# Two-layer hybrid backbone step: layer 1's gates as columns, activation quarters from the halves, four feed-forward chunks

## The chip, the cores and the metric

The kernel runs on 1 core of one Trainium2 chip. The metric is the device time of one execution in microseconds (us). Before the change the median of 3 runs is 1839.01 us (1838.3 to 1839.42).

## The reference, cut to what matters

Two layers work on 640 tokens (128 context tokens and 512 latent tokens, five tiles of 128) of width 1024. Each group has its own conditioning vector (c_ctx and c), so each modulation exists twice.

```
mod = silu(cond) @ ada_w + ada_b            # 6 x 1024: sh_m, sc_m, g_m, sh_f, sc_f, g_f
h = rmsnorm(x, norm_mix) * (1 + sc_m) + sh_m
x = x + g_m * token_mixers(h)               # projections, two kinds of scans, w_out
h = rmsnorm(x, norm_ffn) * (1 + sc_f) + sh_f
gate, up = split(h @ w_up)                  # 2816 hidden features = 22 of 128
x = x + g_f * ((silu(gate) * up) @ w_down)
```

The two gates `g_m` and `g_f` of layer 1 are what the change makes in another place. They do not depend on the tokens.

## The kernel before, in words

**Stages.** `build` runs for each layer the mixer, `w_out` and `ffn`. The large products keep float32 accuracy: each operand is split into a high and a low part (fp32r), and three matmuls (high x high, high x low, low x high) make one. Weights come through `Stream`: SP loads 512 KB into a `raw` buffer, ACT copies the high part `wh` (L103), DVE subtracts to get the low part `wl` (L104). Four slots are cut ahead.

**Order of the work.** The Python program is the order; a scheduler then puts each engine's instructions in a fixed order. Main work yields its cost in model microseconds, and `run` (L184) steps side "lanes" by it: the lane `ada` takes one step for each `Q_ADA` of cost (3.0 in the mixer, 2.0 in `w_out`, 4.0 in `ffn`). `finish` and `drain` run a lane to its end at once. Engines run in order, so an instruction that waits holds all behind it on its engine.

**Modulation.** `ada_cols` (L524) makes shift and scale as columns (one value per partition): for each of 16 tiles it loads 128 rows of the transposed ada_w (512 KB) and runs two DVE multiply-reduces against the broadcast silu rows (L546), 33 lane steps. The gates are needed as rows spread over all partitions, and `ada_gate` (L554) makes them: for each half of 512 columns it accumulates 8 tiles of ada_w on DVE for both conditionings (16 operations, L510 and L512), splits each result (L567 on ACT, L568 on DVE), sums over partitions with two matmuls against ones (L571, L572) and adds the bias (L574 on DVE); 25 lane steps. The mixer starts it for `g_m` after operation r2 (L1062), `ffn` at its start for `g_f` (L1202), and `ffn` needs it before the first chunk's down-projection (L1246).

**Feed-forward.** `ffn` cuts the 22 features into chunks, `CH`: (11, 11) in layer 0, (5, 5, 4, 4, 4) in layer 1. In a chunk the features' activations are made one after the other, and then the chunk's down-projection runs: columns 0 to 511 and 512 to 1023 with `cols_512` (512 wide, L1170 to L1172), and in the last chunk the second half as two `as_` passes of 256 columns (L795 to L797). After each, `x_add` multiplies by the gate row and adds to x (L1113, L1115, DVE). In layer 1 only the first two features are plain (`PLAIN`, L741 and L751); the other 20 use `seven` (L672), a Strassen-Winograd scheme with 7 products in place of 8, 84 matmuls of 320 columns, on combinations of the activation's four quarters (two token halves by two halves of the model width). `combos` (L652) makes these with four full-size additions or subtractions on DVE and splits three of them (E2, E1, E4); `combo_last` (L668) writes the fourth (E3) over a quarter of hT once the plain features have read it.

**Norm.** `norm_b` transposes a normalised tile on TensorE; `norm_c` (L601) scales, shifts and splits it into hT. For layer 1's feed-forward `norm_f` (L621) does that instead, cut at the token half (so tile 2 goes in two pieces), and keeps the unsplit quarters F that `combos` starts from.

**Buffers.** Pool B has 13 buffers, ON 4, PSUM 4 of two banks, the adaLN tiles 2.

Of the kernel before, what the change touches and what calls it, by code (L numbers as in the profile page):

```python
# [10 lines left out]
F32 = mybir.dt.float32  # L11
F32R = mybir.dt.float32r
I32 = mybir.dt.int32
AF = mybir.ActivationFunctionType
ALU = mybir.AluOpType
AX = mybir.AxisListType

P = 128
DM = 1024
KT = DM // P  # L20
NT = 5
TOK = NT * P
HALF = TOK // 2
# [4 lines left out]
NF = DFF // P  # L28
# [3 lines left out]
RAW_BUFS = 3  # L32
W_BUFS = 4
B_BUFS = 13
CH = ((11, 11), (5, 5, 4, 4, 4))
PLAIN = (NF, 2)
HK = KT // 2
LATE = "r2"
# [8 lines left out]
FAST = (0, 1, 3)  # L47
CUT = 256
Q_SCAN = 2.65
Q_ADA = (3.0, 2.0, 4.0)  # L50
ADP_BUFS = 2
BOOT_LOADS = (
    "L00 x4 L01 L10 L02 L11 L12 L13 L03 L20 x2 x3 x0 x1 L21 L30 L22 L31 L32 L33 L23 W W W "
# [94 lines left out]
class Net:  # L148
# [64 lines left out]
    def setup(self):  # L213
        nc, a = self.nc, self.a
        C = self.const
        self.x = C.tile([P, NT, DM], F32, name="x")
        self.ident = C.tile([P, P], F32, name="ident")
        self.onesr = C.tile([P, P], F32R, name="onesr")
        self.mask = C.tile([P, 5, P], I32, name="mask")
        self.rope = C.tile([P, 2, 512], F32, name="rope")  # L220
        self.ncol = C.tile([P, 8], F32, name="ncol")
        self.Dm = C.tile([P, DEPTH, NH, P], F32, name="Dm")
        self.cols = C.tile([P, 64], F32, name="cols")
        self.adab = C.tile([P, 96], F32, name="adab")
        self.lbc = C.tile([P, 2, 8], F32, name="lbc")
        self.oml = C.tile([P, 2, 8], F32, name="oml")
        self.gt = C.tile([P, 5, 16], F32, name="gt")
        self.hp = C.tile([P, 16], F32, name="hp")
        self.ep = C.tile([P, 16], F32, name="ep")
        self.ssq = C.tile([P, NT, 4], F32, name="ssq")  # L230
        self.modc = C.tile([P, DEPTH, 2, 2, 2, 8], F32, name="modc")

        R0 = self.ON("R0")
        nc.sync.dma_start(out=R0[0:8, :P], in_=a["c_ctx"].rearrange("(k p) -> k p", p=P))
        nc.sync.dma_start(out=R0[8:16, :P], in_=a["c"].rearrange("b (k p) -> (b k) p", p=P))
        nc.scalar.dma_start(out=self.ident, in_=a["ident"])
        sr = self.B("sr", F32R)
        self.srv = sr[:, :1024].rearrange("p (k n) -> p k n", k=KT)
        nc.gpsimd.memset(self.hp, -0.5)
        nc.gpsimd.memset(sr[:, :1024].bitcast(F32), 0.0)  # L240
        nc.gpsimd.memset(self.ep, float(np.float32(math.e)))
        warm = self.sm("warm", 1)
        nc.scalar.activation(warm, self.hp[:, :1], AF.Silu)
        nc.scalar.activation(R0[0:16, :P], R0[0:16, :P], AF.Silu)
        R1 = self.R1 = self.ON("R1")
        for r, nm, n, e in ((0, "norm_mix", 16, "l (k p) -> (l k) p"), (16, "norm_ffn", 16, "l (k p) -> (l k) p"),
                            (32, "hgrn_norm", 8, "l (k p) -> (l k) p"), (40, "ret_norm", 8, "l (k p) -> (l k) p"),
                            (48, "hgrn_lb_logits", 16, "l d (k p) -> (l d k) p")):
            nc.gpsimd.dma_start(out=R1[r:r + n, :P], in_=a[nm].rearrange(e, p=P))
        nc.gpsimd.dma_start(out=R1[:96, P:2 * P], in_=a["ada_b"].rearrange("l (k p) -> (l k) p", p=P))  # L250
        self.lgx = C.tile([P, 16], F32, name="lgx")
        nc.gpsimd.dma_start(out=self.lgx, in_=bass.AP(a["ret_decay_logit"].tensor, 0, [[0, P], [1, 16]]))
        nc.gpsimd.dma_start(out=self.ncol, in_=a["ncol"])
        pt = self.ps("pt")
        nc.tensor.transpose(pt[:, :16], R0[:16, :P], self.ident[:16, :16])
        self.sTt = C.tile([P, 16], F32, name="sTt")
        nc.vector.tensor_copy(self.sTt, pt[:, :16])
        self.sT = self.sTt.rearrange("p (c k) -> p c k", c=2)
        skc = self.sTt.rearrange("p (c k) -> p k c", c=2)
        nc.vector.tensor_copy(self.srv[:, :, 0:2], skc)  # L260
        nc.vector.tensor_tensor(self.srv[:, :, 2:4], skc, self.srv[:, :, 0:2].bitcast(F32), op=ALU.subtract)
        self.sel = C.tile([P, 2], F32, name="sel")
        nc.vector.tensor_tensor(self.sel, self.ident[:, 0:2], self.ident[:, 2:4], op=ALU.add)
# [260 lines left out]
    def ada_cols(self, l, m, alloc):  # L524
        V = self.nc.vector
        if self.srow is None:
            self.ada_rows()
            for _ in range(4):
                yield
            for c in range(2):  # L530
                self.pin(self.nc.scalar.activation(self.srow[c], self.srow[c], AF.Silu))  # L531
        tiles = [(which, j) for which in (1, 0) for j in range(KT)]

        def load(which, j):
            w = alloc("adt")
            row = 3072 * m + which * 1024 + j * P
            self.nc.sync.dma_start(out=w[:, :DM], in_=self.a["ada_t"][l, row:row + P])
            return w
        nxt = load(*tiles[0])
        for i, (which, j) in enumerate(tiles):  # L540
            w = nxt
            if i + 1 < len(tiles):
                nxt = load(*tiles[i + 1])
            yield
            for c in range(2):
                r = V.tensor_tensor_reduce(out=self.junk, in0=w[:, :DM], in1=self.srow[c], scale=1.0, scalar=0.0,  # L546
                                           op0=ALU.mult, op1=ALU.add,
                                           accum_out=self.modc[:, l, m, 1 - which, c, j:j + 1])
                if c == 0:
                    self.pin(r)  # L550
            yield
        self.mod_fin(l, m)

    def ada_gate(self, l, m, alloc, out):  # L554
        nc, a = self.nc, self.a
# [44 lines left out]

    def norm_c(self, t, src, l, m):  # L601
        nc = self.nc
        if m == 1 and PLAIN[l] < NF:
            return self.norm_f(t, src, l, m)
        km = KT // 2
        c = 0 if t == 0 else 1
        full = self.ON("full")
# [10 lines left out]
            nc.scalar.copy(hi[:, a:b], fv[:, a:b])  # L618
            nc.vector.tensor_tensor(lo[:, a:b], fv[:, a:b], hi[:, a:b].bitcast(F32), op=ALU.subtract)

    def norm_f(self, t, src, l, m):  # L621
        nc = self.nc
        c = 0 if t == 0 else 1
        sv = src[:, :DM].rearrange("p (k n) -> p k n", k=KT)
        G, S = self.modc[:, l, m, 0, c], self.modc[:, l, m, 1, c]
        a = 0
        while a < P:
            h = (t * P + a) // HALF
            b = min(P, (h + 1) * HALF - t * P)
            n, o = b - a, t * P + a - h * HALF  # L630
            for kh in range(2):
                if (h, kh) not in self.F:
                    self.F[h, kh] = self.B("hf")
                fv = self.F[h, kh].rearrange("p (k n) -> p k n", k=HK)[:, :, o:o + n]
                ks = slice(HK * kh, HK * kh + HK)
                if kh == 0:
                    for k in range(HK):
                        nc.scalar.activation(fv[:, k], sv[:, k, a:b], AF.Identity, bias=S[:, k:k + 1],
                                             scale=G[:, k:k + 1])
                else:  # L640
                    bc = lambda v: v[:, ks].unsqueeze(2).to_broadcast([P, HK, n])
                    nc.vector.tensor_tensor(fv, sv[:, ks, a:b], bc(G), op=ALU.mult)
                    nc.vector.tensor_tensor(fv, fv, bc(S), op=ALU.add)
                hi, lo = (self.hT[:, d, ks, t * P + a:t * P + b] for d in range(2))
                nc.scalar.copy(hi, fv)
                nc.vector.tensor_tensor(lo, fv, hi.bitcast(F32), op=ALU.subtract)
            a = b

    def quarter(self, h, kh):
        return [self.hT[:, d, HK * kh:HK * kh + HK, h * HALF:(h + 1) * HALF] for d in range(2)]  # L650

    def combos(self):  # L652
        V, F = self.nc.vector, self.F
        V.tensor_tensor(F[1, 0], F[1, 1], F[1, 0], op=ALU.subtract)
        V.tensor_tensor(F[0, 0], F[0, 0], F[1, 0], op=ALU.add)
        V.tensor_tensor(F[1, 1], F[0, 0], F[1, 1], op=ALU.subtract)
        V.tensor_tensor(F[0, 1], F[0, 0], F[0, 1], op=ALU.subtract)
        self.E = {}
        for n, q in ((2, (0, 0)), (1, (1, 0)), (4, (0, 1))):
            self.E[n] = [self.B("eh", F32R).rearrange("p (k t) -> p k t", k=HK) for _ in range(2)]  # L660
            self.combo(q, *self.E[n])
# [374 lines left out]
    def mixer(self, l, mid):  # L1036
# [3 lines left out]
        for i, op in enumerate(ORDER):  # L1040
# [18 lines left out]
                ch = self.ret_chain(l, j, QR, vr[nm], on[nm])  # L1059
            self.chains.append(((l, k, j), ch))  # L1060
            if op == LATE:
                self.lanes.append(((l, "gm"), self.ada_gate(l, 0, self.B, self.g_m)))  # L1062
        self.on = [on[n] for n in ("a0", "a1", "b0", "b1")]
        self.oT = [None] * KT
        for u in range(4):
# [133 lines left out]
    def ffn(self, l, mid):  # L1199
        nc = self.nc  # L1200
        self.g_f = []
        self.lanes.append(((l, "gf"), self.ada_gate(l, 1, self.ON, self.g_f)))  # L1202
        if l + 1 < DEPTH:
            for m in range(2):
                self.lanes.append(((l + 1, "c", m), self.ada_cols(l + 1, m, self.ON)))
        f0 = 0
        for ci, nch in enumerate(CH[l]):
# [209 lines left out]
```

## Time and profile before

| | us |
|---|---|
| median of 3 runs | 1839.01 |
| the profiled execution, its own time | 1836.8 |
| its span (first to last instruction) | 1835.0 |
| PE busy | 1767.5 (96%) |
| PE weight load busy | 1676.0 (91%) |
| DVE busy | 1215.7 (66%) |
| ACT busy | 764.0 (42%) |
| mean granted TensorE clock | 0.992 |

PE is TensorE's matmuls, PEld its weight loads, DVE VectorE, ACT ScalarE, SP the engine that issues most DMAs. A row of a group gives count, busy time and the mean of one, and behind the bar the idle time of its engine just before it. A timeline row gives start, duration, engine, line and operation; in brackets stands the idle time before it and who ended it. Matmuls overlap, so the distance of two starts is what one costs, and the duration is longer.

### The profile page before, as it was taken

How to read it: one execution, taken by the hardware profiler on the slowest of the kernel's cores; microseconds unless marked ns; L12 is line 12 of the kernel's file. 1: busy time of each engine (PE TensorE's matmuls, PEld its weight loads, DVE VectorE, ACT ScalarE, POOL GpSimd, SP SyncE). 2: the span in 40 equal slices, each digit the busy share in tenths (PEclk: the TensorE clock that was granted, in tenths of full speed). 3: DMA queues.
4: the chain of work that ended last, by engine and by line, in shares of the span. 5: the costliest groups of instructions: out<-in, count | busy, mean ns of one | idle time of the engine just before them, and what ended most of it. 6: DMA issues, size and time to landing. Idle time of an engine off the chain costs nothing.

```text
span 1835.0 us, 29181 instructions
## 1 busy us (share of the span) xinstructions
PE 1767.5 (96%) x11956; PEld 1676.0 (91%) x11956; DVE 1215.7 (66%) x1905; ACT 764.0 (42%) x1302; POOL 50.6 (3%) x59
## 2 busy tenths in 40 slices
PE   7999999999999999999999999999997799999997
PEld 5999999999999989999999999999896699889896
DVE  6787959755754555554466574776487676777776
ACT  7685545533422112222265464564353133233242
POOL 1100000000000000000000000000000000000000
PEclk9999999999999999999999999999999899999999
DMA  9424232222533444444222112322232223132231
GB/s 341 149 64 132 89 105 94 85 86 59 157 109 110 137 142 129 138 132 132 81 81 64 50 55 69 122 76 76 58 104 92 69 66 101 52 104 69 75 98 58
DMA packets 204358, 184.06 MB, mean 100 GB/s; under 512 B 7376, under 2 KB 171184, under 8 KB 204224
## 3 DMA queue, kind: packets, MB, share of 16 engines
q1 hardware_dynamic: 199328, 179.67, 31.1%
q10 hardware_dynamic: 4640, 2.43, 0.4%
q8 instruction: 94, 1.54, 0.3%
q14 instruction: 40, 0.33, 0.1%
q0 software_dynamic: 256, 0.09, 0.0%
HBM read 177.44 MB, written 4.72 MB: 99 GB/s over the span
## 4 chain that ended last, share of the span: by engine, by line
PE 78%; DVE 12%; ACT 5%; issue 3%; DMA 1%; POOL 1%; SPq 0%; DVEq 0%; POOLq 0%; ACTq 0%
PE gw L751 24%; PE ga L1170 6%; PE ga L1172 6%; PE ga L1171 6%; PE ga L797 4%; PE ga L796 4%; PE ga L795 4%; PE pl L888 3%; PE sx L684 2%; PE sx L685 2%; PE sx L686 2%; DVE wl L104 2%; PE sy L684 2%; PE sy L685 2%; PE sy L686 1%
## 5 line engine op out<-in xcount | busy, mean ns | idle before, releaser
L103 ACT CAST wh<-raw 128x1024 fp32r<-128x1024 f32 (+1 forms) x264 | 264.9, 1004 | 630.6 <-PE ga L1172 212.1
L104 DVE TENSOR_TENSOR wl<-raw,wh 128x1024 fp32r<-128x1024 f32 (+1 forms) x264 | 306.4, 1166 | 258.0 <-ACT wh L103 256.2
L751 PE MATMUL gw<-hT,wh 128*128 128x320 f32 x2432 | 461.9, 311 | 0.0
L751 PEld LDWEIGHTS gw<-hT,wh 128*128 128x128 f32 x2432 | 380.5, 188 | 0.6
L751 PE MATMUL gw<-hT,wl 128*128 128x320 f32 x1216 | 277.2, 309 | 0.0
L751 PEld LDWEIGHTS gw<-hT,wl 128*128 128x128 f32 x1216 | 203.1, 188 | 0.0
L795 PE MATMUL ga<-wh,hT 128*128 128x256 f32 x640 | 185.2, 289 | 0.0
L797 PE MATMUL ga<-wh,hT 128*128 128x256 f32 x640 | 181.3, 283 | 0.0
L796 PE MATMUL ga<-wl,hT 128*128 128x256 f32 x640 | 181.3, 283 | 0.0
L1170 PE MATMUL ga<-wh,act 128*128 128x512 f32 x365 | 145.2, 398 | 0.1
L1171 PE MATMUL ga<-wl,act 128*128 128x512 f32 x365 | 143.1, 392 | 0.0
L1172 PE MATMUL ga<-wh,act 128*128 128x512 f32 x365 | 141.3, 392 | 0.0
L795 PEld LDWEIGHTS ga<-wh,hT 128*128 128x128 f32 x640 | 122.5, 191 | 0.3
L796 PEld LDWEIGHTS ga<-wl,hT 128*128 128x128 f32 x640 | 122.5, 191 | 0.3
L797 PEld LDWEIGHTS ga<-wh,hT 128*128 128x128 f32 x640 | 122.3, 191 | 0.0
L546 DVE CUSTOM_DVE_ANT_0 junk<-adt,srow 128x1024 f32<-128x1024 f32 x96 | 117.1, 1220 | 1.5 <-ACT srow L531 0.2
L1113 DVE TENSOR_TENSOR xa<-ga,gate 128x512 f32<-128x512 f32 (+1 forms) x110 | 62.8, 589 | 41.6 <-PE ga L1172 17.8
L512 DVE SCALAR_TENSOR_TENSOR acc<-adw,sTt,acc 128x512 f32<-128x512 f32 x112 | 79.6, 746 | 15.2 <-DMA adw<-in_ada_w 15.2
L1170 PEld LDWEIGHTS ga<-wh,act 128*128 128x128 f32 x365 | 69.1, 189 | 18.7 <-DVE xa L1113 4.9
L1172 PEld LDWEIGHTS ga<-wh,act 128*128 128x128 f32 x365 | 69.1, 189 | 14.8
L1171 PEld LDWEIGHTS ga<-wl,act 128*128 128x128 f32 x365 | 69.1, 189 | 13.2
L684 PE MATMUL sx<-hT,wh 128*128 128x320 f32 x240 | 76.5, 322 | 3.3 <-DVE sv L694 3.0
(276 smaller groups left out, 3517.8 us busy)
## 6 DMA issues: line engine op xcount, KB each, us to landing
raw<-in_w_in SPq DMA_DIRECT2D x72, 512.0 KB, 3.8
adt<-in_ada_t SPq DMA_DIRECT2D x48, 512.0 KB, 3.8
raw<-in_w_up SPq DMA_DIRECT2D x48, 512.0 KB, 3.7
raw<-in_w_up SPq DMA_DIRECT2D x80, 256.0 KB, 3.0
raw<-in_w_down SPq DMA_DIRECT2D x39, 512.0 KB, 3.6
adw<-in_ada_w SPq DMA_DIRECT2D x64, 256.0 KB, 2.7
adw<-in_ada_w SPq DMA_DIRECT2D x16, 512.0 KB, 10.5
raw<-in_w_out SPq DMA_DIRECT2D x16, 512.0 KB, 3.7
```

Of the source, the lines that this page charges most:

```text
L103: nc.scalar.copy(hi[:, :n], raw[:, :n])
L104: nc.vector.tensor_tensor(lo[:, :n], raw[:, :n], hi[:, :n].bitcast(F32), op=ALU.subtract)
L512: nc.vector.scalar_tensor_tensor(d, w, s, d, op0=ALU.mult, op1=ALU.add)
L546: r = V.tensor_tensor_reduce(out=self.junk, in0=w[:, :DM], in1=self.srow[c], scale=1.0, scalar=0.0, op0=ALU.mult, op1=ALU.add, accum_out=s ...
L684: mm(o, hi[:, k], h[0][:, k], start=first and k == 0, stop=False, skip_group_check=True)
L751: mm(o, w[:, k], self.hT[:, d, k, sl], start=k == 0 and i == 0, stop=k == KT - 1 and i == 2)
L795: mm(o, a_hi, hi[:, j], start=i == 0, stop=False)
L796: mm(o, a_hi, lo[:, j], start=False, stop=False)
L797: mm(o, a_lo, hi[:, j], start=False, stop=i == nk - 1)
L1170: mm(o, a_hi, hi[:, j], start=i == 0, stop=False)
L1171: mm(o, a_hi, lo[:, j], start=False, stop=False)
L1172: mm(o, a_lo, hi[:, j], start=False, stop=i == nk - 1)
```

## The change

Layer 1's two gates are made in layer 0's feed-forward as columns: `ada_cols` gets two further passes (m = 2 and 3, 8 tiles each) into a new tile `gcol`. In layer 1 `gate_rows` spreads them: per conditioning 8 float32 matmuls of 128 columns, whose stationary operand is a column repeated 128 times and whose moving operand is the identity, and one ACT copy from PSUM. `ada_gate` remains for layer 0. `norm_f` is gone; `combos` makes the four quarters by adding high and low part of hT. Layer 1 has four chunks, and the `ada` lane in `ffn` steps at 3.4.

```
-CH = ((11, 11), (5, 5, 4, 4, 4))
+CH = ((11, 11), (6, 6, 5, 5))
-Q_ADA = (3.0, 2.0, 4.0)
+Q_ADA = (3.0, 2.0, 3.4)
+        self.gcol = C.tile([P, 2, 2, 8], F32, name="gcol")
@@ ada_cols
-        tiles = [(which, j) for which in (1, 0) for j in range(KT)]
+        if m >= 2:
+            m -= 2
+            tiles = [(2, j) for j in range(KT)]
+        else:
+            tiles = [(which, j) for which in (1, 0) for j in range(KT)]
...
-                                           accum_out=self.modc[:, l, m, 1 - which, c, j:j + 1])
+                                           accum_out=(self.gcol[:, m, c, j:j + 1] if which == 2 else
+                                                      self.modc[:, l, m, 1 - which, c, j:j + 1]))
...
-        self.mod_fin(l, m)
+        if which == 2:
+            b = 48 * l + 24 * m + 16
+            for c in range(2):
+                V.tensor_tensor(self.gcol[:, m, c], self.gcol[:, m, c], self.adab[:, b:b + 8], op=ALU.add)
+        else:
+            self.mod_fin(l, m)
+
+    def gate_rows(self, m, alloc, out):
+        nc = self.nc
+        for c in range(2):
+            pg = self.ps("pg")
+            for j in range(KT):
+                nc.tensor.matmul(pg[:, j * P:(j + 1) * P], self.gcol[:, m, c, j:j + 1].to_broadcast([P, P]),
+                                 self.ident, start=True, stop=True)
+            yield
+            g = alloc("gate")
+            out.append(g)
+            nc.scalar.copy(g[:, :DM], pg)
+            yield
@@ norm_c
-        if m == 1 and PLAIN[l] < NF:
-            return self.norm_f(t, src, l, m)
-    def norm_f(self, t, src, l, m):
...
@@ combos
         V, F = self.nc.vector, self.F
+        for q in ((1, 1), (1, 0), (0, 0), (0, 1)):
+            F[q] = self.B("hf")
+            hi, lo = self.quarter(*q)
+            V.tensor_tensor(F[q].rearrange("p (k t) -> p k t", k=HK), hi.bitcast(F32), lo.bitcast(F32), op=ALU.add)
@@ mixer
-                self.lanes.append(((l, "gm"), self.ada_gate(l, 0, self.B, self.g_m)))
+                self.lanes.append(((l, "gm"), self.ada_gate(l, 0, self.B, self.g_m) if l == 0 else
+                                    self.gate_rows(0, self.B, self.g_m)))
@@ ffn
-        self.lanes.append(((l, "gf"), self.ada_gate(l, 1, self.ON, self.g_f)))
+        self.lanes.append(((l, "gf"), self.ada_gate(l, 1, self.ON, self.g_f) if l == 0 else
+                            self.gate_rows(1, self.ON, self.g_f)))
         if l + 1 < DEPTH:
-            for m in range(2):
+            for m in range(4):
                 self.lanes.append(((l + 1, "c", m), self.ada_cols(l + 1, m, self.ON)))
```

## Rows read from the trace of the kernel before

**Rows 1.** The page, part 1: busy time, share of the span, instructions.

```profile
PE 1767.5 (96%) x11956; PEld 1676.0 (91%) x11956; DVE 1215.7 (66%) x1905; ACT 764.0 (42%) x1302; POOL 50.6 (3%) x59
```

**Rows 2.** Stretches: start:end, length, PE, PEld, DVE, ACT, POOL, clock, DMA, GB/s.

```profile
467.00:910.00 443.00, 441.53 (x2757) 420.68 (x2756) 239.12 (x336) 107.51 (x141) 0.12 (x1) 1.00 0.40 125
...
1344.80:1361.40 16.60, 13.80 (x106) 13.23 (x106) 15.35 (x32) 9.82 (x25) 1.41 (x2) 1.00 0.36 112
...
1378.00:1390.00 12.00, 7.70 (x49) 6.91 (x48) 12.00 (x16) 3.97 (x6) 0.00 (x0) 1.00 0.22 66
...
1402.00:1411.00 9.00, 8.49 (x50) 8.12 (x50) 4.83 (x8) 2.63 (x4) 0.00 (x0) 0.86 0.10 30
...
1433.70:1444.50 10.80, 0.07 (x2) 0.02 (x1) 9.50 (x15) 2.27 (x4) 0.00 (x0) 0.73 0.56 176
...
1470.00:1820.00 350.00, 348.50 (x2041) 316.29 (x2040) 250.64 (x367) 119.14 (x177) 0.66 (x1) 1.00 0.24 74
```

**Rows 3.** Waits of PE, 1340 to 1470: total us, times, longest.

```profile
PE pg L571 <- ACT hl L567: 17.6, 4, 10.7
PE pt L598 <- DVE xn L1192: 2.8, 2, 2.5
PE sy L685 <- DVE hT L666: 2.7, 1, 2.7
PE sx L684 <- DVE sv L694: 1.7, 2, 1.2
```

**Rows 4.** Timeline of PE, layer 1's first chunk.

```profile
1385.38 0.41 PE L685 MATMUL sy<-hT,wh 128*128 128x320 f32 x1 [2.74 <-DVE hT L666]
...
1400.77 0.59 PE L571 MATMUL pg<-hl,onesr 128*128 128x512 f32 x1 [2.60 <-ACT hl L567]
...
1403.99 0.47 PE L684 MATMUL sy<-hT,wh 128*128 128x320 f32 x1
1404.26 0.40 PE L685 MATMUL sy<-hT,wh 128*128 128x320 f32 x1
...
1452.58 0.39 PE L1170 MATMUL ga<-wh,act 128*128 128x512 f32 x1
...
1463.00 0.39 PE L1171 MATMUL ga<-wl,act 128*128 128x512 f32 x1
```

**Rows 5.** Timeline of PE: where each of layer 1's chunks begins its `seven`.

```profile
1378.18 0.31 PE L684 MATMUL sx<-hT,wh 128*128 128x320 f32 x1
...
1482.90 0.30 PE L684 MATMUL sx<-hT,wh 128*128 128x320 f32 x1
...
1582.03 0.30 PE L684 MATMUL sx<-hT,wh 128*128 128x320 f32 x1
...
1661.43 0.30 PE L684 MATMUL sx<-hT,wh 128*128 128x320 f32 x1
```

**Rows 6.** Chain that ended last, layer 1's mixer: 8 float32 products of 128 columns.

```profile
1050.59 1.78 PE pu L921 x16
```

**Rows 7.** Groups on DVE, 1314 to 1452.4: count, busy us, mean ns.

```profile
L512 DVE SCALAR_TENSOR_TENSOR acc<-adw,sTt,acc 128x512 f32<-128x512 f32 x28 | 20.0, 745 | 1.6 <-DMA adw<-in_ada_w 1.6
...
L654 DVE TENSOR_TENSOR hf<-hf 128x1280 f32<-128x1280 f32 x1 | 1.5, 1492 | 0.0
```

**Rows 8.** Waits of PE, 1140 to 1320 (layer 1's mixer after r2).

```profile
PE po L932 <- DVE S L941: 1.0, 1, 1.0
PE pd L879 <- DVE QS L847: 1.0, 1, 1.0
```

**Rows 9.** Groups on DVE, 467 to 910 (layer 0's feed-forward).

```profile
L546 DVE CUSTOM_DVE_ANT_0 junk<-adt,srow 128x1024 f32<-128x1024 f32 x64 | 78.2, 1221 | 1.1
```

**Rows 10.** A stretch at the end of layer 0's feed-forward.

```profile
900.00:920.00 20.00, 20.00 (x170) 20.00 (x169) 9.05 (x19) 5.87 (x15) 1.10 (x2) 1.00 0.27 80
```

**Rows 11.** Timeline of DVE, the end.

```profile
1822.47 1.28 DVE L1283 SCALAR_TENSOR_TENSOR y<-x,rs,nf 128x1024 f32<-128x1024 f32 x1 [0.44 <-POOL rs L592]
...
1824.94 1.28 DVE L1283 SCALAR_TENSOR_TENSOR y<-x,rs,nf 128x1024 f32<-128x1024 f32 x1 [0.40 <-POOL rs L592]
```

More of the change, by code (lines that the diff above doesn't have):

```diff
@@ L619, in norm_c @@
             nc.vector.tensor_tensor(lo[:, a:b], fv[:, a:b], hi[:, a:b].bitcast(F32), op=ALU.subtract)
-    def norm_f(self, t, src, l, m):
[L622 to L647, printed above, removed]
     def quarter(self, h, kh):
```

## The prediction

> **What bounds the kernel now.** I read the page first: PE is busy 96% of the span, DVE 66% [rows 1], so time can only come from the few places where PE stands, or from matmuls that fall away. The stretches show where those places are [rows 2]: in layer 0's feed-forward (467 to 910) PE lacks 1.5 of 443 us, in layer 1's from 1470 to 1820 again 1.5 of 350. But layer 1's norm (1344.8 to 1361.4) lacks 2.8 of 16.6 us, and its first chunk is full of holes: 1378 to 1390 has 7.7 busy of 12 us, and from 1433.7 to 1444.5 PE does nothing at all. The waits of PE name the cause [rows 3]: 17.6 us in four waits of the gate's spreading matmuls (L571) for the split of the DVE sums (L567), the longest 10.7. PE is in order, so all of `seven` and the down-projection stand behind them. Smaller: 2.8 us on the norm's transposes, 2.7 on E3 (L666), 1.7 on `seven`'s own differences.
>
> The stall has a second price. After the wait of 2.60 us at 1400.77, starts of the 320-column matmuls lie 0.27 us apart (1403.99 to 1404.26) [rows 4], and the granted clock of that stretch is 0.86, a mix of the level of 1.2 and that of 2.4 GHz; in the long hole it is 0.73 [rows 2].
>
> How much the first chunk loses in all is read from where the chunks begin [rows 5]. The second (5 features) takes 1582.03 - 1482.90 = 99.13 us, the third (4) 79.40, so a feature costs 19.73 and a chunk 0.5 besides. A down-projection matmul of 512 columns costs (1463.00 - 1452.58) / 46 = 0.227 us [rows 4], where 46 is the count of starts between; a feature has 30 of them, 6.8 us, so a `seven` is 12.9. The first chunk has 3 of these and 5 features to project: 38.8 + 34.0 + 0.5 = 73.3 us. It takes 1482.90 - 1378.18 = 104.7. **Lost: 31.4 us**, with the eight spreading matmuls and the slow clock in it.
>
> **The change, part by part.**
>
> *Gate out of layer 1's feed-forward.* 28 L512 operations, 20.0 us of DVE [rows 7], four L510 and the splits leave DVE there, 16 loads leave SP's queue, and PE no longer waits for L567: -31.4 us, if nothing takes the place.
>
> *Spreading by small matmuls.* A gate has 2 x 8 float32 matmuls of 128 columns. Eight such take 16 passes and 1.78 us in the mixer [rows 6], so a gate adds 3.6 us to PE. That their stationary operand is one column repeated the trace does not show; the bounds are 0, when all of it falls into the norm's 2.8 us of idle PE, and 7.1, twice the rate. I take 3.6, since the nearest row has the same type and shape: **+3.6**. They wait for nothing late, only for a PSUM buffer. The Trainium skill ("TensorE: Matmul & The Clock Gate", section Back-to-back issue gap) gives about 81 ns for a matmul of 128 columns in a stream with weight loads; by it the 32 passes would take 2.6 us instead of 3.6, and the two gates together 2 us less. The measured row is kept.
>
> *Quarters from the halves.* `combos` gets four more additions of 1280 columns at 1.49 us [rows 7], 6.0 us of DVE ahead of E2 and E3. DVE is busy 12.0 of 12.0 us in 1378 to 1390 [rows 2], so this is no free cover. Against it about ten of the removed L512 (0.745 each) and two L510 stood between the norm's end and E3, some 8 us, and `norm_f`'s extra piece falls away (some 0.6 us of DVE, more on ACT). So E3 comes about 2 us earlier than now, its wait shrinks from 2.7 to about 1, and the wait on L694 (1.2 at most) and two small ones remain: I take **+3.0** for what is left of stalls. Bounds: 0, and 11, when the removed work turns out to have been hidden and E3 comes 6.0 us later (2.7 + 6.0) with some twenty matmuls at the low level behind it (20 x 0.12, the 0.27 less a `seven`'s mean of 12.9 / 84 = 0.15). The norm itself: -0.5 (bounds -2.8 and +3, an addition slipped ahead of a tile's chain).
>
> *Layer 1's mixer.* The same 3.6 us of matmuls come, eight spreading matmuls of 0.227 go (-1.8), and of PE's waits after r2, most of them for DVE [rows 8], one of 1.0 and some more should go, since 28 L512 leave DVE there too: -1.3. Together **+0.5** (bounds -2 and +2.5).
>
> *Layer 0's feed-forward.* 32 more multiply-reduces, at 1.22 us each [rows 9], 39 us. DVE is busy 239 of 443 us and would be 278; PE hardly waits there [rows 2], so this is **0** in the body, and what hides it is DVE's idle half. The 16 loads of 512 KB equal in bytes the 32 of 256 KB that leave layer 1; they go through SP before the weight loads, with DMA share 0.40 now. The end is the place to look: the lane has 25 + 33 + 33 + 17 + 17 = 125 steps, and the model cost until `drain` is 44 x 6.53 + 3 x 34.65 + 19.65 = 411, so 120.8 steps at 3.4. Two tiles are left and run in a burst, 2 x 2 x 1.22 = 5 us of DVE, ahead of the first x_add of the last pass. In that stretch DVE has 11 of 20 us free [rows 10]. Without the cover the norm of layer 1's mixer starts 5 us late. I take **+0.7** (0 to 5).
>
> *Four chunks.* The number of matmuls stays. A border costs 0.5 us (above), and ten x_adds leave a DVE that is not the bound: **-0.4**. B's 13 buffers are then just full (six E halves, six activations, one gate half); the next activation takes the place of one that the down-projection has read early, so 0. In the tail DVE is the bound: a tile every 2.47 us (1822.47 to 1824.94) [rows 11]. With 5 instead of 4 features the last pass starts 4 x 3 matmuls earlier, by an estimate of half the 512-column price 1.4 us; one feature more in 256-column form takes some of it: **-1.1** (0 to -1.4).
>
> **Sum:** -31.4 + 3.6 + 3.0 - 0.5 + 0.5 + 0.7 - 0.4 - 1.1 = -25.6. The profiled execution took 1836.8 us (span 1835.0), so 1811.2. The median lies 2.2 above it; I carry that over: **1813 us**.
>
> **Rivals.**
>
> *B, a stall in place of the stall.* DVE stays full through the first two `seven`: four additions, four differences, four splits (12 x 1.49 = 18 us) and the cuts of the first `seven` slots must pass between the norm and 1390. Then PE waits for E2, E3 and L694, 5 to 14 us more than I took, or the norm's transposes wait because the gate's matmuls hold the fourth PSUM buffer while three projections hold the others. For it: DVE busy 12.0 of 12.0 us [rows 2]. Against it: more work leaves this stretch than enters. It gives 1818 to 1827. The clock is part of this: the wait of 2.74 us at 1385.38 is followed by a stretch at 1.00, that of 2.60 by one at 0.86 [rows 2, 4], so the same length can cost nothing or some 1.5 us. The Trainium skill ("TensorE: Matmul & The Clock Gate", section Why this matters for your kernels) says that idle gaps between bursts put the array back to half its clock. By that rule B's every longer wait pays twice; the trace agrees after the L571 waits and not after the one for E3.
>
> *C, the relief goes further.* The spreading falls into the norm's idle PE, the remaining waits vanish with DVE's load: 7 to 9 us better, 1803 to 1807. For it: the steady chunks lose only 1.5 of 350 us. Against: E3 comes late even in my count.
>
> *D, the drain, slower than before.* If the lane does not keep up and most of the 16 new tiles are still to do at `drain`, each is 2.44 us of DVE in front of the last pass's x_add and the norms of layer 1. With 11 us free there [rows 10], it eats the 25.6 us gained when more than (25.6 + 11) / 2.44 = 15 tiles are left; all 16 and their loads in turn give 1841 to 1850. For it: the queue is in order. Against: the count leaves 2, and DVE has nearly half its time free.
>
> *E, no difference:* it would need B at its worst and D in part, 1836 to 1842.
>
> **How the numbers follow.** Forecast 0.64 (1807 to 1818), B 0.20, C 0.10, D 0.04, E 0.02. The likeliest gives 1813. The range goes from C's low end to most of B: 1803 to 1824. About 0.2% (3.7 us) is what a measurement of this kernel can tell from no change: faster 0.94, same 0.02, slower 0.04.
>
> **What would show it.** Right: no wait of a spreading matmul above 1 us in layer 1, the first chunk's four `seven` at about 13 us each, clock near 1.00 throughout layer 1's feed-forward, L512 gone from there, 32 more L546 before 910 with PE still full, three borders less one. Wrong: a hole of PE of more than 5 us between the norm and the third `seven` (B); L546 bursts after 905 and PE waiting in layer 1's first projections (D); waits for PSUM before L598. The forecast fails if the 31.4 us were not the gate's: the first chunk, now 4 `seven` and 6 features to project, should take 4 x 12.9 + 6 x 6.8 + 0.5 = 93 us and the 3.0 of stalls; above 105 the cause was another.

## The result, and the profile after

The changed kernel takes 1818.83 us (median of 4 runs, 1817.08 to 1820.04), the kernel before 1838.65 beside it: **ratio 0.9893, 95% interval 0.9875 to 0.991, 19.8 us faster**. The forecast was 1813 with a range of 1803 to 1824, a gain of 25.6. The direction and the main term held, but 6 us of the gain are missing, and by the prediction's own list the time lies just inside rival B's range (1818 to 1827) and 0.8 us outside the forecast's own (1807 to 1818). The runs below show where the 6 us went, and that the change left 15 us to be had.

The profiled execution took 1819.22 us (span 1817.4; before 1836.8 and 1835.0). The page's first part, which answers to [rows 1]: DVE has 20 us less work, and PE is as busy as it was, in a shorter span.

```profile
PE 1767.6 (97%) x12019; PEld 1680.8 (92%) x12019; DVE 1196.1 (66%) x1874; ACT 764.2 (42%) x1293; POOL 50.6 (3%) x59
```

Stretches of the changed kernel (columns as in [rows 2]): layer 0's feed-forward, its end, then layer 1's from its norm on. The cut at 1386.4 is where `seven` begins, that at 1488 where the second chunk's does.

```profile
467.00:910.00 443.00, 441.51 (x2755) 420.33 (x2754) 270.55 (x393) 107.68 (x141) 0.66 (x1) 1.00 0.44 139
900.00:920.00 20.00, 20.00 (x168) 19.89 (x166) 16.38 (x33) 5.21 (x13) 0.55 (x1) 1.00 0.57 175
...
1346.70:1386.40 39.70, 35.62 (x242) 34.98 (x241) 25.04 (x36) 16.34 (x30) 2.02 (x2) 0.96 0.09 27
1386.40:1488.00 101.60, 95.03 (x512) 84.82 (x511) 70.31 (x92) 34.04 (x43) 0.00 (x0) 0.95 0.24 73
1488.00:1800.00 312.00, 311.02 (x1855) 285.56 (x1854) 218.24 (x319) 110.29 (x164) 0.00 (x0) 1.00 0.25 76
```

Layer 0 carries the 28 multiply-reduces that fall before 910 for nothing (441.5 of 443 us busy, as in [rows 2]). Of layer 1's feed-forward nearly all that PE still loses lies between 1346.7 and 1488: 4.1 and 6.6 us without work, and 1.0 behind. Its waits from 1340 to 1490 (engine, line, waited for: total us, times, longest), against [rows 3]: the 17.6 us on the split of the gate's sums are gone. Two waits stood there before and are shorter, that for the norm's xn (2.8, now 0.3) and that for E3's low part (2.7, now the 1.6 on L664, hT). The other five are new.

```profile
PE gw L738 <- DVE full L637: 2.8, 1, 2.8
PE sx L682 <- ACT eh L663: 2.3, 1, 2.3
PE sy L682 <- ACT hT L663: 1.8, 1, 1.8
PE sy L683 <- DVE hT L664: 1.6, 1, 1.6
PE pt L622 <- DVE full L637: 0.9, 1, 0.9
PE sx L683 <- DVE eh L664: 0.8, 1, 0.8
PE pt L622 <- DVE xn L1191: 0.3, 1, 0.3
```

Where the four chunks begin `seven`, against [rows 5]:

```profile
1386.46 0.31 PE L682 MATMUL sx<-hT,wh 128*128 128x320 f32 x1
...
1488.00 0.30 PE L682 MATMUL sx<-hT,wh 128*128 128x320 f32 x1
...
1606.42 0.30 PE L682 MATMUL sx<-hT,wh 128*128 128x320 f32 x1
...
1705.19 0.30 PE L682 MATMUL sx<-hT,wh 128*128 128x320 f32 x1
```

With the first up-projection matmul of layer 1 (1344.87 before, 1346.70 after) these split the difference of the two spans, -17.6 us:

| stretch | before | after | difference |
|---|---|---|---|
| up to layer 1's first up-projection | 1344.87 | 1346.70 | +1.8 |
| from there to the first `seven` (norm, spread) | 33.31 | 39.76 | +6.45 |
| first chunk (3 `seven`, 5 projections; now 4 and 6) | 104.72 | 101.54 | -3.2 |
| all other chunks and the tail | 352.1 | 329.4 | -22.7 |

A sixth feature in the first chunk takes 20.05 us off the others (91.4 - 71.35, the first chunks of runs 1 and 6 below), so the last two lines are -23.2 for the stall and -2.7 for the border and the tail.

**Two lists.** VectorE between the norm and the second product of `seven` (start, us, engine, line, operation, tiles; in brackets the idle time before it and what ended that):

```profile
1361.32 1.38 DVE L641 TENSOR_TENSOR hT<-full,hT 128x512 fp32r<-128x512 f32 x2
1372.21 1.23 DVE L104 TENSOR_TENSOR wl<-raw,wh 128x1024 fp32r<-128x1024 f32 x1 [9.52 <-ACT wh L103]
...
1378.26 1.49 DVE L651 TENSOR_TENSOR hf<-hT 128x1280 f32<-128x1280 f32 x1
...
1381.67 4.29 DVE L651 TENSOR_TENSOR hf<-hT 128x1280 f32<-128x1280 f32 x3
...
1392.82 4.28 DVE L664 TENSOR_TENSOR eh<-hf,eh 128x1280 fp32r<-128x1280 f32 x3
```

The halves are complete when L641 ends at 1362.7; the four additions (L651) need nothing else. But on VectorE's list a weight's split (L104) stands ahead of them. It waits for ScalarE's copy L103, which waits for a buffer that PE still reads. So VectorE idles 9.5 us with ready work behind, and then four additions, four differences and four splits are all late at once (run 1 below moves the additions alone). The Trainium skill ("Perfetto Trace Analysis", section Tensor Engine Instruction (MATMUL, LD_WEIGHTS)) says that ScalarE and VectorE take their instructions strictly first in, first out; the 9.52 us agree.

PE in the norm, the same columns, and then ScalarE:

```profile
1350.99 1.95 PE L570 MATMUL pg<-ident,gcol 128*128 128x128 f32 x16
1356.71 1.09 PE L622 MATMUL pt<-ident,xn 128*128 128x128 f32 x8 [0.90 <-DVE full L637]
1360.64 0.39 PE L738 MATMUL gw<-hT,wh 128*128 128x256 f32 x1 [2.84 <-DVE full L637]
```

```profile
1357.84 0.46 ACT L635 ACTIVATE full<-pt,modc 128x128 f32<-128x128 f32 x1 [2.79 <-PE pt L622]
...
1358.70 1.16 ACT L635 ACTIVATE full<-pt,modc 128x128 f32<-128x128 f32 x3
1359.74 1.02 ACT L575 COPY gate<-pg 128x1024 f32<-128x1024 f32 x1
```

The spread for the first conditioning is done at 1352.9, but its copy out of PSUM (L575) starts at 1359.74: on ScalarE's list the last norm tile's activations stand first, and they wait for transposes that PE has not made. The buffer is taken for 8.8 us before its copy even starts, and the third projection has none until L637 empties another at 1360.6: PE waits 2.84 us, and its granted clock in 1360 to 1380 is 0.91.

### The profile page after: what moved, and what is told of

Read it like the earlier page. It is cut to its first block, busy times and chain, and to the rows that moved or that the text cites. A ratio compares the mean times of both kernels' runs of the same rounds, so it can differ in the third digit from the quotient of the medians.

```text
span 1817.4 us, 29233 instructions
## 1 busy us (share of the span) xinstructions
PE 1767.6 (97%) x12019; PEld 1680.8 (92%) x12019; DVE 1196.1 (66%) x1874; ACT 764.2 (42%) x1293; POOL 50.6 (3%) x59
## 4 chain that ended last, share of the span: by engine, by line
PE 81%; DVE 10%; ACT 4%; issue 2%; DMA 1%; POOL 1%; SPq 0%; POOLq 0%; DVEq 0%; ACTq 0%
PE gw L749 25%; PE ga L1169 6%; PE ga L1171 6%; PE ga L1170 6%; PE ga L795 4%; PE ga L794 4%; PE ga L793 4%; PE pl L886 3%; PE sx L682 3%; PE sx L683 2%; PE sx L684 2%; PE sy L682 2%; PE sy L683 2%; PE sy L684 2%; DVE wl L104 1%
## 5 line engine op out<-in xcount | busy, mean ns | idle before, releaser
L103 ACT CAST wh<-raw 128x1024 fp32r<-128x1024 f32 (+1 forms) x265 | 265.3, 1001 | 632.0 <-PE ga L1171 195.1
L104 DVE TENSOR_TENSOR wl<-raw,wh 128x1024 fp32r<-128x1024 f32 (+1 forms) x265 | 306.7, 1162 | 267.8 <-ACT wh L103 265.8
L551 DVE CUSTOM_DVE_ANT_0 junk<-adt,srow 128x1024 f32<-128x1024 f32 x128 | 156.1, 1219 | 2.7 <-DMA adt<-in_ada_t 0.8
L1169 PE MATMUL ga<-wh,act 128*128 128x512 f32 x360 | 141.8, 394 | 0.0
L1171 PE MATMUL ga<-wh,act 128*128 128x512 f32 x360 | 138.8, 389 | 0.0
L886 PE MATMUL pl<-X 128*128 128x128 f32 x560 | 72.9, 277 | 5.2 <-ACT X L873 5.1
L886 PEld LDWEIGHTS pl<-X 128*128 128x128 f32 x560 | 67.7, 191 | 7.8 <-ACT X L873 7.4
## 6 DMA issues: line engine op xcount, KB each, us to landing
adw<-in_ada_w SPq DMA_DIRECT2D x16, 512.0 KB, 10.5
```

What stands on the lines that cost most here:

```text
L103: nc.scalar.copy(hi[:, :n], raw[:, :n])
L104: nc.vector.tensor_tensor(lo[:, :n], raw[:, :n], hi[:, :n].bitcast(F32), op=ALU.subtract)
L886: nc.tensor.matmul(pl[:, i * P:(i + 1) * P], X[:, TOK + i * P:TOK + (i + 1) * P], X[:, i * P:(i + 1) * P], start=True, stop=True)
L1169: mm(o, a_hi, hi[:, j], start=i == 0, stop=False)
L1171: mm(o, a_lo, hi[:, j], start=False, stop=i == nk - 1)
```

## The experiments

All times are medians; the ratio is to the kernel before on the same chip, with its 95% interval. "Norm" is the stretch from the first up-projection matmul of layer 1 to its first `seven`, "first chunk" the one from there to the second chunk's.

**1. The additions early.** The four additions move out of `combos` into a function `halves`, which is issued behind the last norm tile (the differences stay in `combos`; the move itself is left out here):

```diff
...
@@ ws
             while mid and hf and self.pend:
                 self.flush1()
+            if mid and hf and self.after_norm:
+                self.after_norm.pop(0)()
@@ ffn
+                if PLAIN[l] < NF:
+                    self.after_norm.append(self.halves)
                 yield from self.ws(*evs[:3], mid=mid)
```

> The changed kernel with one move: the four additions that make the quarters from the halves are issued right behind the last norm tile, ahead of the three plain units' weight cuts on VectorE's list. In the changed kernel VectorE stood idle for 9.52 us (1362.7 to 1372.2) behind a weight cut while the additions' inputs lay ready, and the first chunk lost 8.5 us beyond its matmuls. Theory (order of the list): the additions and the first differences fill that gap, the four waits of TensorE at the first unit of seven products (2.33, 1.77, 0.82 and 1.64 us) and the half clock behind them go, first chunk 101.5 us to 93 to 96, time 1812.5 us (1810 to 1815). Rival (too much work: VectorE's 6 us of additions are one load too many wherever they stand): the waits only change their place, no more than 2 us better, 1817 us or over.

Measured: 1809.03 us, ratio 0.9834 (0.9821 to 0.9848). The norm stays long, 40.4 us, and the first chunk falls from 101.5 to 91.4, read from where the first two chunks begin `seven`:

```profile
1387.14 0.31 PE L686 MATMUL sx<-hT,wh 128*128 128x320 f32 x1
...
1478.56 0.30 PE L686 MATMUL sx<-hT,wh 128*128 128x320 f32 x1
```

PE's waits from 1340 to 1490 are those of the norm alone, and one of 0.3:

```profile
PE gw L742 <- DVE full L638: 2.8, 1, 2.8
PE pt L623 <- DVE full L638: 0.9, 1, 0.9
PE pt L623 <- DVE xn L1197: 0.3, 1, 0.3
PE sx L686 <- DVE sv L696: 0.3, 1, 0.3
```

So 10 us were the place on the list and not the work: the same 6 us of additions cost nothing here. The gain came out larger than the 8.5 us of the expectation, since a first chunk without a hole takes 91.4 us and not the 93 that I had reckoned: the changed kernel lost 10.1.

**2. The spread late.** The feed-forward gate's lane of layer 1 starts behind the last norm tile (the hook in `ws` is that of run 1, but takes all that is listed):

```diff
...
@@ ffn
-        self.lanes.append(((l, "gf"), self.ada_gate(l, 1, self.ON, self.g_f) if l == 0 else
-                            self.gate_rows(1, self.ON, self.g_f)))
+        if l == 0:
+            self.lanes.append(((l, "gf"), self.ada_gate(l, 1, self.ON, self.g_f)))
+        else:
+            self.after_norm.append(lambda: self.lanes.append(((l, "gf"), self.gate_rows(1, self.ON, self.g_f))))
```

> The changed kernel with one move: the feed-forward gate's spread in layer 1 (16 matmuls, then ScalarE's copy, twice) is put on its lane only after the last norm tile's transposes are issued. Theory (a PSUM buffer: the first spread took one at 1351 and ScalarE emptied it only at 1360.7, so the last transposes came late, TensorE waited 0.90 and 2.84 us, and the clock fell): the stretch from the first up-projection matmul to the first seven products falls from 39.8 us to 36 to 37.5, time 1816 us (1814.5 to 1818). Rival (the stretch is long because of the 32 matmuls alone, 3.9 us, which only move): no difference within 1 us, 1818 to 1820.

Measured: 1816.02 us, 0.987 (0.9857 to 0.9884); norm 37.56, first chunk 101.8. Here it is the other way round than in run 1: L738's 2.8 is gone, the waits of `seven` stay. The 0.9 on L637 is gone too, and the transposes wait 1.9 for xn instead.

```profile
PE sx L683 <- ACT eh L664: 2.3, 1, 2.3
PE pt L623 <- DVE xn L1195: 1.9, 2, 1.6
PE sy L683 <- ACT hT L664: 1.8, 1, 1.8
PE sy L684 <- DVE hT L665: 1.6, 1, 1.6
PE sx L684 <- DVE eh L665: 1.0, 1, 1.0
```

**3. Both moves**, the diffs of runs 1 and 2 together.

> Both moves together. If the two losses are separate, they add: about 1809.5 us (1806.5 to 1812). If the later spread lands on the stretch that the earlier additions need (the second spread, its copies on ScalarE and the splits of the quarters), the sum is smaller, and it comes out no better than the early additions alone.

Measured: 1806.06 us, 0.9817 (0.9803 to 0.983); norm 36.26, first chunk 91.4. The two losses are separate: the single gains of 9.8 and 2.8 us add up to the 12.8 of both.

**4. ScalarE's list or the buffer?** The spread stays in the norm, but its copy is issued with it:

```diff
@@ gate_rows
                                  self.ident, start=True, stop=True)
-            yield
             g = alloc("gate")
```

> The changed kernel with ScalarE's copy of the gate's spread issued in the same step as its matmuls, so that on ScalarE's list it stands ahead of the last norm tile's activations and not between them; the spread itself stays in the norm. Theory (the loss in the norm is ScalarE's list: ready since 1352.9, the copy stood behind activations that waited for the very transposes that lacked a buffer): the waits of 0.90 and 2.84 us go, as with the later spread, 1816 us (1814.5 to 1817.5). Rival (a buffer taken in the norm costs that much whoever empties it when): 1818 to 1820.

Measured: 1814.58 us, 0.9866 (0.9853 to 0.988); norm 35.29, first chunk 102.6. The copy now runs ahead of the last tile's activations, 5.9 us earlier:

```profile
1353.80 1.02 ACT L574 COPY gate<-pg 128x1024 f32<-128x1024 f32 x1
```

The 2.84 us are gone, the 0.90 before L622 are not: those do not hang on the copy, and in this the expectation was wrong. A buffer taken in the norm is harmless when it is emptied at once. The edit also takes a step out of the lane, so the second spread comes earlier (1359.75 against 1367.23); it does not stand in the place of the 2.84 us, where PE now runs projections. That the first chunk is 1.1 us longer than in the changed kernel is not explained.

**5. Additions early and copy at once**, the diffs of runs 1 and 4 together, the best kernel with the quarters:

> The early additions and the copy at once, together: 1805.5 us (1803.5 to 1807.5) if both losses are places on a list and nothing else; at least 1808 if the spread in the norm still delays the additions.

Measured: 1803.67 us, 0.981 (0.9796 to 0.9823); norm 35.28, first chunk 90.6: both losses are gone, 15 us under the change. Its VectorE in the same place, and a stretch of it and of the changed kernel over the same 11.5 us:

```profile
1361.38 0.69 DVE L641 TENSOR_TENSOR hT<-full,hT 128x512 fp32r<-128x512 f32 x1 [0.68 <-ACT hT L640]
1362.10 5.70 DVE L651 TENSOR_TENSOR hf<-hT 128x1280 f32<-128x1280 f32 x4
1367.72 1.22 DVE L104 TENSOR_TENSOR wl<-raw,wh 128x1024 fp32r<-128x1024 f32 x1
```

```profile
1360.70:1372.20 11.50, 11.50 (x72) 11.50 (x71) 10.79 (x9) 5.07 (x6) 0.00 (x0) 1.00 0.16 47
```

```profile
1360.70:1372.20 11.50, 11.50 (x71) 11.50 (x72) 1.99 (x3) 3.29 (x6) 0.00 (x0) 0.85 0.00 1
```

The first stretch is this kernel's (VectorE 10.79 us busy, clock 1.00), the second the changed kernel's (1.99, 0.85).

**6. The gates alone.** The kernel before with `gcol`, `gate_rows` and the lane's 3.4; `norm_f` and the old `combos` and `CH` stay. Against the changed kernel:

```diff
-CH = ((11, 11), (6, 6, 5, 5))
+CH = ((11, 11), (5, 5, 4, 4, 4))
...
@@ norm_c, with norm_f of the kernel before
+        if m == 1 and PLAIN[l] < NF:
+            return self.norm_f(t, src, l, m)
@@ combos
-        for q in ((1, 1), (1, 0), (0, 0), (0, 1)):
-            F[q] = self.B("hf")
-            hi, lo = self.quarter(*q)
-            V.tensor_tensor(F[q].rearrange("p (k t) -> p k t", k=HK), hi.bitcast(F32), lo.bitcast(F32), op=ALU.add)
```

> The kernel before with the gate columns and their spread alone: five chunks, and the quarters still written by the norm itself. If the gate's 64 accumulations, its hl sinks and its pg waits are the whole loss of 31.4 us in layer 1's first chunk, and the spread costs what it cost in the changed kernel (6.4 us in the norm, 1.3 us in the mixer and the drain), this gives 1838.9 - 31.4 + 6.4 + 1.3 + 1 to 4 of leftover stall = 1815 to 1819 us, and so about all of the change's gain. If the quarters were needed to free VectorE as well, it stays at 1823 us or over.

Measured: 1806.07 us, 0.9827 (0.9813 to 0.9842), 32 us faster than before and 12 faster than the whole change. The expectation, which added the changed kernel's 6.4 us in the norm, was too high: here ScalarE's list has the copy at 1353.27, the norm takes 35.08, and between 1340 and 1455 PE waits for nothing but the transposes:

```profile
PE pt L622 <- DVE xn L1217: 1.0, 2, 0.7
```

Its first chunk of 5 features takes 71.35 us, so the kernel before lost 104.7 - 71.35 = 33.4 there:

```profile
1381.77 0.31 PE L708 MATMUL sx<-hT,wh 128*128 128x320 f32 x1
...
1453.12 0.30 PE L708 MATMUL sx<-hT,wh 128*128 128x320 f32 x1
```

**7. Four chunks alone.**

```diff
-CH = ((11, 11), (5, 5, 4, 4, 4))
+CH = ((11, 11), (6, 6, 5, 5))
```

> The kernel before with four chunks (6, 6, 5, 5) in layer 1 and nothing else. Theory: one border less and a longer last chunk, worth what they were in the changed kernel (-1.3 and -1.7 us): 1836 us (1834.5 to 1838). Rival: a sixth unit of seven products in the first chunk gives the overloaded VectorE 19.7 us more of TensorE's work to hide the gate behind, and part of the 31.4 us goes without any gate columns: 1825 to 1833 us.

Measured: 1834.48 us, 0.9978 (0.9969 to 0.9988). The first chunk takes 125.55 us where 91.4 would do without a hole, so it loses 34.1, no less than before: the longer chunk hides nothing of the gate, although its spreading waits shrink:

```profile
PE pg L571 <- ACT hl L567: 13.4, 4, 6.0
PE sy L685 <- DVE hT L666: 3.1, 1, 3.1
```

**8. Quarters alone.** The kernel before with the hunks of `norm_c` and `combos` of run 6 the other way round; gates and chunks as before.

> The kernel before with the quarters made by additions from the halves and nothing else. Theory: VectorE is what the first chunk waits for, so the four additions of 1.48 us cost near their time, less what the split norm saves: +2 to +6 us, 1841 to 1845 us. Rival: they stand in idle time and the norm is shorter: -3 to +1 us, 1836 to 1840 us.

Measured: 1844.19 us, 1.0034 (1.0022 to 1.0046), slower by 5 to 6 us (1838.87 beside it). The split of E2 is a new wait:

```profile
PE pg L571 <- ACT hl L567: 17.9, 4, 11.1
PE sx L658 <- ACT eh L639: 5.1, 1, 5.1
```

**9. A late drain.** The changed kernel, with the lane of layer 0's feed-forward stepped every 4.0:

```diff
-Q_ADA = (3.0, 2.0, 3.4)
+Q_ADA = (3.0, 2.0, 4.0)
```

> The changed kernel with the lane of layer 0's feed-forward stepped every 4.0 us of matmul work instead of every 3.4. About 22 of the lane's steps, some 11 weight tiles with 22 multiply-reduces of 1.22 us (27 us of VectorE), are then left for the drain ahead of layer 1. Theory (VectorE carries them out in order, ahead of the additions that the last five tiles of TensorE, some 17.7 us, feed): TensorE loses 27 - 17.7 = 9 us or more, 1828 us (1824 to 1836). Rival (TensorE's buffers and ScalarE cover the drain): 1818 to 1821 us, as the changed kernel.

Measured: 1836.89 us, 0.9991 (0.9982 to 1.0): the whole gain is gone. 22 multiply-reduces follow 910 where the changed kernel has four. Stretches of this kernel, then the timeline: the first xn of layer 1's first norm on VectorE, and the transposes on PE that wait for it:

```profile
920.00:930.00 10.00, 1.62 (x14) 1.42 (x12) 9.96 (x25) 1.02 (x4) 2.67 (x3) 0.68 0.49 153
930.00:940.00 10.00, 0.00 (x0) 0.00 (x0) 9.76 (x17) 0.00 (x0) 0.00 (x0) 0.50 0.58 191
```

```profile
939.48 0.75 DVE L1191 TENSOR_SCALAR xn<-x,rs 128x1024 f32<-128x1024 f32 x1
...
940.28 1.97 PE L622 MATMUL pt<-ident,xn 128*128 128x128 f32 x8 [18.66 <-DVE xn L1191]
```

The cost is higher than either theory had it. 18 more multiply-reduces, one every 1.27 us, are 23 us of VectorE, and layer 1's first up-projection starts 19.7 us later (1366.41): the last pass covers 3 us of them. The trace shows why so little: on VectorE's list the x_adds stand among the multiply-reduces and were done by 926, but the norm's first xn stands behind 19 of the 22. Its factor was ready at about 921.8 (GpSimd), it ran at 939.48. PE ran out at about 922 and waited 18.7 us for it. This is the same loss as in run 1, a ready instruction behind others on a list.

**10. The change without its quarters** (gates and four chunks, `norm_f` kept: the diff of run 6 but for `CH`).

> The change without its quarters: gate columns, spread and four chunks, and the norm still writes the quarters itself. If the parts add, 1806.1 (gates alone) less the border and the tail (1.3 + 1.7 us, as in the changed kernel): 1803 us (1801.5 to 1804.5), and the quarters from the halves then cost the changed kernel some 16 us, not the 5.3 us that they cost the kernel before. If the four chunks need the space or the time that the quarters give, 1805 us or over.

Measured: 1804.76 us beside 1840.73 of before, 0.981 (0.9796 to 0.9823). Against 0.9893 the quarters cost the changed kernel 0.8%, some 15 us; alone they cost 5 to 6. The kernel before is 1.9 us slower on this chip than in run 6; with that taken off, the parts add as expected. And the ratio equals that of experiment 5: well placed, the quarters cost nothing.

**11. The same with the spread late**, by the diff of run 2.

> The same with the feed-forward gate's spread put on its lane only behind the last norm tile. With the gates alone ScalarE emptied the first spread's buffer at once (2.3 us after its matmuls began, against 8.8 us in the changed kernel) and TensorE waited only 1.0 us in the norm, so theory: no more than 1 us better, 1802 us (1801 to 1804). Rival (any PSUM buffer taken during the norm costs the 3 us of the late spread in the changed kernel): 1799 to 1801 us.

Measured: 1807.18 us, 0.9819 (0.9806 to 0.9833), no better than run 10, and over both expectations. Where the copy comes at once, there is nothing to gain by moving the spread. In the trace the norm even grows, from 35.07 to 38.17 us, and PE waits 2.8 us for xn where it waited 1.0: the early spread had filled a part of that wait.

## Why the prediction was right, and where its terms were off

- **Gate out of layer 1's feed-forward, -31.4.** Right: the kernel before lost 33.4 us there (run 6), and the gates alone give more than the whole change. Undersized by 2, since a first chunk without holes takes 71.35 us and not 73.3. Some 1.4 us of this lie in the border: the last six matmuls of a chunk's down-projection run behind the next chunk's first six of `seven` (1.39 us from 1453.99 in run 6), so a middle chunk gets six from the one before it and the first chunk gets none.
- **"What is left of stalls", +3.0.** This is the term that failed: 10.1 us. The step said that L512 and L510 stood "between the norm's end and E3, some 8 us", that their going makes room, and so E3 comes "about 2 us earlier". VectorE did get the room, 9.52 us of it, but idled through it, because the additions stand behind a weight's split (run 1). I took a free engine for one that takes whatever is ready. PE starts on E3's low part 12.8 us after the first matmul of `seven`, where it was 7.2 before [rows 4, 5], so E3 comes 5.6 us later and not 2 earlier:

```profile
1399.30 0.63 PE L683 MATMUL sy<-hT,wh 128*128 128x320 f32 x1 [1.64 <-DVE hT L664]
```

  10.1 lies inside the bounds given (0 to 11), and the upper bound's "E3 comes 6.0 us later" is near the 5.6, though for another reason than the one given there. The price of the clock was in it as foreseen: from 1390.7 to 1403.0 there are 27 matmuls, 4.2 us at the 0.154 of a clean `seven`, at a granted clock of 0.58:

```profile
1390.70:1403.00 12.30, 8.05 (x27) 7.08 (x28) 11.11 (x12) 5.25 (x5) 0.00 (x0) 0.58 0.00 1
```

  Its 8.1 us and the wait of 2.33 just ahead make 10.5, about the loss read from the chunks.
- **Spread and norm, +3.6 - 0.5.** This term failed too: it came to +6.45. With the copy at once it is 35.29 - 33.31 = +2.0, so the rest of the term was rather too high; the other 4.5 us were ScalarE's list. The 2.0 agree with a spread of 2 x 1.71 us of which a part ran in time that PE had idle, as C had said: the norm's wait for xn is 0.3 us where it was 2.8, and the 0.9 on L637 came. "They wait for nothing late, only for a PSUM buffer" looked at how they get a buffer and not at when it is emptied. Rival B named the buffer ("the norm's transposes wait because the gate's matmuls hold the fourth PSUM buffer"), though what waited 2.84 us was a projection, but priced it inside its 5 to 14 us, and I left it out of the sum.
- **Layer 1's mixer and the drain, +0.5 + 0.7.** +1.8 at layer 1's first up-projection, 0.5 of it already there at layer 0's (461.25 against 460.71): +1.3, in agreement, but runs 10 and 11, which are alike up to there, differ by 1.9 at that point. Two tiles were left at the drain, as counted.
- **Layer 0's body, 0.** Right: VectorE is busy 270.6 us before 910 where 278 was reckoned, 5 of that behind 910, and PE is unchanged.
- **Four chunks and the tail, -0.4 - 1.1.** -2.7 in the trace, -4 alone (run 7, interval -2.2 to -5.7): right in sign, too small.
- **Rivals.** The outcome is the forecast's gain with B's stall in it, and the time is in B's range. B's sign, a hole of more than 5 us before the third `seven`, is there in pieces: 6.6 us in four waits, none above 2.4. The waits of B's kind cost 14.6 us in the two places. VectorE was full there, as B said (11.11 of 12.3 us), but only because it had idled 9.52 us before: run 1 has the same work and no such waits. C's time is that of runs 5 and 10. D's mechanism is real but its price was wrong: "with 11 us free there" only 3 us of the added drain are covered, and 11 tiles at the drain, not more than 15, eat 18 of the gain of 19.8 us (run 9).

The sum by measured terms is +1.8 + 6.45 - 33.4 + 10.1 - 2.7 = -17.7, against -17.6 between the spans. So the terms of the forecast were off by 8.0 us together, +7.1 of it the stalls and +3.4 the norm, less 3.2 by which the gate and the chunks gave more. That the median is off by only 5.8 is luck: the profiled execution of the kernel before was 2.2 us faster than its median, which the forecast carried over, and the one of the changed kernel was not. And the range held because it took in most of B, not because the forecast's own 1807 to 1818 did.

## What to carry to other kernels

Room that an edit makes on an engine is worth something only to the instruction that is next on that engine's list: look what stands ahead of the work that is to use it, and what that waits for. A buffer's cost is the time until it is emptied, so issue the copy with the matmuls that fill it, ahead of anything that waits for a later result of the same engine. And when a change has parts, time each alone and all but each: here one part cost 15 of the 35 us that the others gave.

## What the hardware showed that I had not expected

- Four waits of 2.33, 1.77, 0.82 and 1.64 us, with one, one and eleven matmuls between them, go with a granted clock of 0.58 over 12.3 us, near the level of 1.2 GHz. The Trainium skill ("TensorE: Matmul & The Clock Gate", section Why this matters for your kernels) warns of idle gaps between bursts, and the 0.58 agrees. The length of one wait does not tell the outcome here: those of 2.60 us (before) and 2.84 us (after) are followed by stretches at 0.86 and 0.85, that of 2.74 (before) by one at 1.00 [rows 2, 4].
- In the hole of run 9, without a single matmul from 930 to 940, the clock shows 0.50, and one 18.7-us wait was paid nearly in full by the span (+17.6).
- A float32 product whose stationary operand is one column repeated costs what one with stored operands costs. The 1.78 us of [rows 6] are the part of a product on the chain; the timeline of the kernel before has the same 1.95 us as the spread in the changed kernel, and from start to next start the two take 1.70 us (1050.43 to 1052.13) and 1.71 us (1350.99 to 1352.70), about 107 ns for each of 16 passes. The 81 ns of the Trainium skill (the same page, section Back-to-back issue gap) would make it 1.3 us; it does not hold for this form.

```profile
1050.43 1.95 PE L921 MATMUL pu<-va,kT 128*128 128x128 f32 x16
```
